# One encoder layer on eight cores: the order of all instructions fixed beforehand by a list scheduler, attention probabilities as the stationary operand, weights packed in blocks

## The chip, the cores and the metric

The kernel runs on all 8 cores of one Trainium2 chip, two dies of four cores each. Every core works on its own data; there is no collective. The time of an execution is the device time of the slowest core, in microseconds (us).

In some executions the cores of one die show a lower granted TensorE clock, and the time is longer.

## The reference

One layer of a streaming encoder. Core c handles prompt stream c (2048 tokens) and two running streams of 64 tokens each, 2176 tokens in all, with D = 1024, 16 heads of 64, and an FFN width of 2816.

```python
mod = silu(c) @ w_ada + b_ada                      # 9 vectors: shift, scale, gate
x = x + 0.5*gt1 * swiglu(modulate(rmsnorm(x)), w_ffn1_in, w_ffn1_out)
h = modulate(rmsnorm(x), ...); z = h @ w_in        # Q K V f B C X GA GC
logit[t,s] = q_t.k_s/8 + sum(log f_j, s < j <= t)  # causal, plus a cache of 1024 rows
o_attn = softmax(logit) @ v                        # for the two running streams
o_conv = B * short_conv(C * X, width 3)            # causal, per channel
m = sigmoid(GA)*o_attn + sigmoid(GC)*o_conv
x = x + gt2 * (m @ w_out)
x = x + 0.5*gt3 * swiglu(modulate(rmsnorm(x)), w_ffn2_in, w_ffn2_out)
y = rmsnorm(x)                                     # K, V, log f and conv states are outputs too
```

## The kernel before

The instructions of each engine are issued in the order in which the Python program emits them. Heads are handled in 8 pairs, and each pair c also owns 128 channels of the conv branch. The projections of the next pair and the conv work are "side" items, taken from a queue between the steps of attention (cuts are marked with `...`):

```python
def maybe_side():                     # called between the steps of attention
    ...
    while side_q and (n0 + (pushed[0] - p0) - len(side_q)) < int(2.4*nside*step[0]/88.0):
        side(1)

# scores: keys stationary; exp on ScalarE; P@V: V stationary, 512 query columns move
act(PT[pi][:, lo:512], PB[sb_][:, lo:512], AF.Exp, ..., bias=NF[...], scale=1.0)
mm([(PB[ob][:, lo:512], va[:, i, hh, :], PT[pi][:, lo:512], i == 0, i == ntile - 1)], ...)

def normalize(ob, ...):               # V has 64 ones columns, so rows 64..127 hold the sum
    act(LND[64:128, 0:ncol], PB[ob][64:128, 0:ncol], AF.Ln, ...)
    act(RD[64:128, 0:ncol], LND[64:128, 0:ncol], AF.Exp, ..., scale=-1.0)
    ...                               # VectorE: multiply, then times the gate

def sigmoid_split(dst, src_ps, ...):  # three ScalarE passes for each gate
    return [act(dst, src_ps, AF.Exp, scale=-1.0), act(dst, dst, AF.Ln, bias=1.0),
            act(dst, dst, AF.Exp, scale=-1.0)]

def wcols(w, c0, n):                  # a weight block: rows of 128 f32 = 512 bytes
    return w.rearrange("(k p) n -> p k n", p=128)[:, :, c0:c0 + n]
```

K and V outputs go through three staging buffers to DRAM. x is written to DRAM (xs) before attention and read back by five large loads after it.

The softmax here doesn't subtract the row's maximum and nothing guards it: scores larger than these inputs give would overflow.

## Time and profile before

The median is 2667.99 us of 3 executions (2651.4 to 2799.87; the last, 5.6% above the first, is a slow one). The profile is of core 1, span 2679.1 us.

These are lines of the page: the span, busy time and instruction counts of each engine, and the DMA packets.

```profile
span 2679.1 us, 35551 instructions; the slowest of 8 cores (2629.1 to 2679.1 us)
PE 2083.8 (78%) x11881; PEld 1013.9 (38%) x11881; DVE 920.9 (34%) x1566; ACT 967.3 (36%) x1948; POOL 258.9 (10%) x338
DMA packets 307537, 137.12 MB, mean 51 GB/s; under 512 B 255472, under 2 KB 278128, under 8 KB 307344
```

PE is TensorE, PEld its weight loads, ACT ScalarE, DVE VectorE. The next lines are windows of the same trace: start and end, length, busy time (and instructions) of each engine, mean granted clock of TensorE, share of the DMA engines, GB/s. They are the starved start of FFN 1, attention, the output projection, and FFN 2.

```profile
core 1: us, PE busy (x) PEld busy (x) DVE busy (x) ACT busy (x) POOL busy (x), PEclk, DMA share, GB/s
118.00:252.00 134.00, 118.86 (x986) 61.73 (x987) 23.32 (x46) 20.07 (x37) 58.54 (x70) 0.91 1.29 114
...
800.00:2000.00 1200.00, 864.49 (x5125) 435.20 (x5123) 476.87 (x833) 622.07 (x1312) 87.10 (x113) 0.84 0.37 34
2000.00:2140.00 140.00, 99.05 (x413) 41.48 (x414) 57.87 (x99) 57.04 (x102) 7.00 (x8) 0.84 0.52 92
2140.00:2600.00 460.00, 450.34 (x2384) 215.35 (x2382) 114.27 (x184) 68.45 (x126) 36.25 (x50) 0.99 0.26 34
```

Nearly half of the time is attention, where TensorE is busy 72% of the time and gets a clock of 0.84. What it waits for is in the list of TensorE's waits (engine, operand, line, what ended the wait: total us, times, longest):

```profile
PE pb L330 <- ACT RG L340: 125.9, 105, 6.2
...
PE pb L330 <- DVE stg L798: 67.5, 12, 25.2
...
PE pb L330 <- DMA wsall<-w_in: 44.4, 6, 11.4
```

The first are exponentials. `stg` are the staging buffers of K and V: a projection can't be drained until an earlier write to DRAM has landed. The list of DMA issues shows how late these writes and the weights land (last number: median us from issue to landing):

```profile
wsall<-w_in POOLq DMA_DIRECT2D x64, 256.0 KB, 14.2
...
wsall<-w1o POOLq DMA_DIRECT2D x22, 256.0 KB, 4.5
kT<-stg SPq DMA_DIRECT2D x22, 256.0 KB, 14.1
```

A w_in block has 512-byte rows and a w1o block 4 KB rows. Both are 256 KB, and the first takes three times as long (14.2 against 4.5 us). The loads convert 512-byte f32 rows to 256-byte bf16 rows, and 255472 of 307537 packets are under 512 B.

### The profile page before, as it was taken

To read this page: it belongs to the slowest core of one execution; us is meant where nothing else is said; L and a number is where in the kernel's file an instruction comes from. 1 tells how busy PE (TensorE), PEld (TensorE's weight loads), DVE (VectorE), ACT (ScalarE), POOL (GpSimd) and SP (SyncE) were. 2 spreads that over 40 slices of the span, in tenths; PEclk is the share of its full clock that TensorE was granted. 3 is DMA by queue.
4 is the path that set the end of the run, shared out by engine and by line. 5 is a ranking of instruction groups with operands and counts; after the bars stand their busy time and mean duration, and the time that the engine had idled before them with its cause. 6 is when DMAs were issued, how large, how long until landed. Compare 5 with 4: busy or idle time off the path is not lost.

```text
span 2679.1 us, 35551 instructions; the slowest of 8 cores (2629.1 to 2679.1 us)
## 1 busy us (share of the span) xinstructions
PE 2083.8 (78%) x11881; PEld 1013.9 (38%) x11881; DVE 920.9 (34%) x1566; ACT 967.3 (36%) x1948; POOL 258.9 (10%) x338
## 2 busy tenths in 40 slices
PE   1598999988477877766684677777857699999986
PEld 0244444433144343433333334343323344444433
DVE  0411232233554443343433344443334422222233
ACT  3611101123344646445362454636643411001111
POOL 2243011000010100000010000100010110010000
PEclk9898999998688887878887888888878899999988
DMA  9899316202563352626417342241236332162111
GB/s 188 81 127 129 47 17 62 33 32 80 48 75 37 23 59 18 57 22 31 37 20 54 17 42 33 26 57 18 21 64 125 32 40 32 16 60 32 20 63 71
DMA packets 307537, 137.12 MB, mean 51 GB/s; under 512 B 255472, under 2 KB 278128, under 8 KB 307344
## 3 DMA queue, kind: packets, MB, share of 16 engines
q0 software_dynamic: 260688, 80.79, 36.9%
q1 hardware_dynamic: 46672, 54.05, 6.4%
q8 instruction: 101, 1.65, 0.3%
q14 instruction: 76, 0.62, 0.1%
HBM read 179.70 MB, written 35.82 MB: 80 GB/s over the span
## 4 chain that ended last, share of the span: by engine, by line
PE 61%; DMA 14%; DVE 9%; ACT 8%; issue 6%; SPq 1%; DVEq 0%; ACTq 0%; POOL 0%; POOLq 0%
PE pb L330 61%; DMA kT<-stg 5%; ACT RG L340 4%; DMA kT<-wsall 3%; DVE tmp L441 3%; DMA wsall<-w_in 2%; DMA wsall<-w1i 2%; DMA RX<-xT 1%; ACT scr L340 1%; ACT RX L340 1%; ACT lnms L340 1%; DMA RX<-xs 1%; DVE RX L769 1%; DVE RX L492 1%; ACT H L340 1%
## 5 line engine op out<-in xcount | busy, mean ns | idle before, releaser
L330 PE MATMUL pb<-H,wsall 128*128 128x512 bf16 (+1 forms) x5800 | 1220.1, 363 | 122.4 <-DMA wsall<-w_in 44.4
L330 PEld LDWEIGHTS pb<-H,wsall 128*128 128x128 bf16 x5800 | 537.3, 101 | 706.9 <-issue 223.6
L330 PE MATMUL pb<-RG,wsall 128*128 128x512 bf16 (+2 forms) x2416 | 546.4, 368 | 125.4 <-DVE RX L492 46.8
L340 ACT ACTIVATE RG<-pb,NF 128x512 bf16<-128x512 f32 (+3 forms) x640 | 369.2, 626 | 301.8 <-PE pb L330 299.7
L330 PEld LDWEIGHTS pb<-RG,wsall 128*128 128x128 bf16 x2416 | 232.2, 103 | 402.9 <-issue 210.6
L340 ACT ACTIVATE scr<-pb 128x512 bf16<-128x512 f32 (+1 forms) x220 | 117.1, 533 | 718.6 <-PE pb L330 718.6
L475 DVE TENSOR_TENSOR RG<-pb,scr 128x512 bf16<-128x512 f32 (+1 forms) x220 | 134.1, 611 | 523.0 <-PE pb L330 509.9
L330 PE MATMUL pb<-RG,RX 128*128 128x64 bf16 (+4 forms) x592 | 137.5, 305 | 121.1 <-ACT RG L340 96.8
L492 DVE SCALAR_TENSOR_TENSOR RX<-pb,DER,RX 128x512 f32<-128x512 f32 (+1 forms) x192 | 112.6, 594 | 217.1 <-PE pb L330 213.8
L340 ACT ACTIVATE scr<-RX 128x512 bf16<-128x512 f32 (+1 forms) x160 | 81.8, 556 | 270.2 <-PE pb L330 224.5
L330 PE MATMUL pb<-wsall,H 128*128 128x128 bf16 x1088 | 87.6, 250 | 105.0 <-DVE stg L798 40.4
L319 POOL DMA_DIRECT2D wsall<-w_in x65 | 57.1, 884 | 908.9 <-PE pb L330 908.9
L330 PE MATMUL pb<-RX 65*128 65x64 bf16 (+4 forms) x592 | 129.7, 313 | 17.0 <-DVE RX L954 17.0
L330 PE MATMUL pb<-RX,wsall 65*128 65x512 bf16 (+1 forms) x336 | 119.0, 401 | 8.6 <-DVE RX L954 8.6
L330 PE MATMUL pb<-scr,ones_bf 128*128 128x512 bf16 (+1 forms) x160 | 59.4, 400 | 82.5 <-ACT scr L340 77.5
L330 PEld LDWEIGHTS pb<-wsall,H 128*128 128x128 bf16 x1088 | 80.9, 114 | 108.9 <-issue 107.5
L330 PEld LDWEIGHTS pb<-RG,RX 128*128 128x128 bf16 x592 | 46.7, 108 | 186.0 <-issue 171.6
L441 DVE SCALAR_TENSOR_TENSOR tmp<-RX,DER,pb 128x512 f32<-128x512 f32 (+1 forms) x144 | 85.2, 592 | 68.3 <-ACT pb L340 48.0
L903 DVE TENSOR_TENSOR tmp<-pb,tmp 64x64 f32<-64x64 f32 (+1 forms) x96 | 50.6, 527 | 144.1 <-ACT tmp L340 142.6
L340 ACT ACTIVATE H<-tmp,MOD 128x512 bf16<-128x512 f32 (+1 forms) x144 | 85.8, 597 | 33.2 <-DVE tmp L441 28.6
L340 ACT ACTIVATE RG<-pb,NFS 128x64 bf16<-128x64 f32 x288 | 87.0, 313 | 22.7 <-ACT RG L340 1.5
L340 ACT ACTIVATE lnms<-pb 64x64 f32<-64x64 f32 (+3 forms) x116 | 55.6, 479 | 97.8 <-PE pb L330 96.2
(90 smaller groups left out, 1189.3 us busy)
## 6 DMA issues: line engine op xcount, KB each, us to landing
wsall<-w_ada POOLq DMA_DIRECT2D x72, 256.0 KB, 18.2
wsall<-w_in POOLq DMA_DIRECT2D x64, 256.0 KB, 14.2
wsall<-w1i POOLq DMA_DIRECT2D x44, 256.0 KB, 10.5
wsall<-w2i POOLq DMA_DIRECT2D x44, 256.0 KB, 7.1
RX<-xT SPq DMA_DIRECT2D x4, 2048.0 KB, 27.8
xs<-RX SPq DMA_DIRECT2D x4, 2048.0 KB, 6.8
RX<-xs SPq DMA_DIRECT2D x4, 2048.0 KB, 29.0
wsall<-w1o POOLq DMA_DIRECT2D x22, 256.0 KB, 4.5
```

Source lines behind the costliest of these rows:

```text
L319: P.dma("gpsimd", lambda e, d=dst, s=src_ap: e.dma_start(out=d, in_=s), writes=[WSB[i]], sem=WSS[i])
L330: ins = e.matmul(o, lhsT=l, rhs=r, start=st, stop=sp)
L340: return P.op("scalar", lambda e: e.activation(out=out, in_=in_, func=func, **kw), reads=reads, writes=writes)
L441: P.op("vector", lambda e, k=k, i=i, lo=lo, ln_=ln_, seq=seq: e.scalar_tensor_tensor(out=TMP[i][:, lo:lo + ln_], in0=xv[:, k, t0 + lo:t0 + ...
L475: P.op("vector", lambda e, ia=ia, bb=bb, jj=jj, t0=t0, n=n: e.tensor_tensor(out=gv[:, jj, t0:t0 + n], in0=PB[bb][:, 0:n], in1=SAB[ia][:, 0 ...
L492: P.op("vector", lambda e, bank=bank, mo=mo, t0=t0, lo=lo, ln_=ln_, seq=seq: e.scalar_tensor_tensor(out=xv[:, mo, t0 + lo:t0 + lo + ln_], ...
L769: P.op("vector", lambda e, r0=r0, lo=lo, ln_=ln_: e.tensor_tensor(out=T1[r0:r0 + 64, lo:lo + ln_], in0=T1[r0:r0 + 64, lo:lo + ln_], in1=T2 ...
L903: P.op("vector", lambda e: e.tensor_tensor(out=TT[r0:r0 + 64, 0:ncol], in0=PB[ob][0:64, 0:ncol], in1=RD[64:128, 0:ncol], op=ALU.mult), rea ...
```

## The change

The intent is to let a planner find the overlap that was interleaved by hand, and to take work off ScalarE and the DMA queues. The diff has about 2480 lines; this is its core.

```diff
-def mm(items, reads, writes): return P.op("tensor", fn, reads, writes)   # issued as emitted
+n.prio = self.base + self.step * 1e-3 + (prio or 0.0)   # every operation is a node
+P.schedule()                                            # one fixed order for every engine
...
+for c in range(8):                     # smaller number = more urgent
+    P.at(300.0 + c*10 + 5); kvqga(c + 1)   # projections of the next pair
+    P.at(300.0 + c*10);     attend(c)
+    P.at(500.0 + c*10);     conv(c)
...
+p_a = Pool("a", banks[0:4], excl=True)     # PSUM: scores
+p_o = Pool("o", banks[4:6], excl=True)     # P@V
+p_p = Pool("p", banks[6:8], excl=True)     # every projection, and the transposes
...
-mm([(PB[ob][:, lo:512], va[:, i, hh, :], PT[pi][:, lo:512], ...)])       # V stationary
+mm([(ot.ap[:, s*66:s*66+65], pt.ap[:, s*128:(s+1)*128], va[:, i, hh, 0:65], ...)
+    for s in subs])                        # P stationary: 64 columns of V and one of 2.0
-act(..., AF.Ln, ...); act(..., AF.Exp, scale=-1.0)
+dve(reciprocal(...)); dve(tensor_tensor(...))           # normalisation on VectorE
-sigmoid_split(...)                                      # Exp, Ln, Exp
+act(..., AF.Tanh, scale=0.5)    # the ones column of 2.0 absorbs the factor 0.5
-P.dma("gpsimd", ... w_in.rearrange("(k p) n -> p k n", p=128)[:, :, c0:c0+128])
+P.dma("gpsimd", ... w_in[block])   # [64, 128, 1024], packed beforehand: 4 KB rows
```

How the planner places an operation: it keeps a modelled time for each engine, takes the most urgent operation that is ready, gives it a free slot of its pool, and advances the engine to the time when that slot is free:

```python
n = heapq.heappop(rdy[e])[2]            # most urgent ready operation of engine e
got, full = slot_for(n)                 # a slot that no tile holds; it may be free only later
...
st = max(avail[e], n.ready)
for t, s in zip(n.alloc, got):
    ...
    st = max(st, s.free_at)             # the engine waits for the slot
avail[e] = st + occ
```

x is still written to DRAM, and comes back as 40 small tiles just before each is used. The conv branch of a pair runs on TensorE's projection banks with this chain on VectorE for each block of 512 tokens: C times X, the three taps, times B, times the gate, add.

## The prediction

> **What bounds the kernel now.** By the busy-time windows of the profiled core (span 2679 us):
>
> | us | stage | PE busy | granted clock |
> |---|---|---|---|
> | 0-118 | loads, first norm | under half | 0.87-1.00 |
> | 118-587 | FFN 1 | 92-100% | 1.00 once fed |
> | 587-800 | its tail, gate sums, first K/V | 64% | 0.82 |
> | 800-2000 | attention, projections | 73% | 0.84 |
> | 2000-2140 | output projection | 75% | 0.83-0.89 |
> | 2140-2680 | FFN 2, tail | 92% | 0.81-0.99 |
>
> Where TensorE is fed, a matmul costs its columns: 16 of 128 columns took 0.89 us (56 ns each), eight of 64 took 0.23 us (29 ns each). Weight loads hide. [...] By this law before needs about 1825 us at full clock (estimate: 1779 us of columns, 11881 matmuls); some 850 us are waiting and the lower clock that goes with it. The waits of PE between 690 and 2000 us: exponentials 126 us, K/V staging buffers 133 us (12 to 25 us at a time at the start of a head pair, until their write to DRAM is done), w_in loads 44 us.
>
> **What changes.**
> - PE work barely shrinks. P-stationary P@V is 2176 matmuls of 65 columns, about 65 us at 29-30 ns, against 118 us before; token-major gate and transposes give some back. Estimate for after: 1780 us at full clock.
> - ACT loses the Ln/Exp normalisation (93 us) and three-pass sigmoids (about 130 us; one tanh pass, about 45, instead). Eight 64-column exponentials (313 ns each) become one of 512 plus a DVE add. I estimate ACT 505 us and DVE 445 us in attention, against PE 705: TensorE is the bound if the schedule feeds it.
> - Packed weights: a block with 512-byte rows lands in 14-18 us, one with 4 KB rows (w1o) in 4.5 us. This removes two waits of 23 and 25 us from the chain in FFN 1, the 44 us in attention, and the slow landing of the kT writes in the same queues (14 us).
> - Scheduling: norm, gate sums, first K/V, output projection and FFN 2's start overlap.
>
> **Sum of after** (estimates): start 72 (was 118); FFN 1 515 (about 570); attention and projections 830, namely 705 at clock 0.96 and 88% fed (about 1310 with the gate stage); output projection 80 (140); FFN 2 495 and tail 15 (540). Total about 2010 us.
>
> **Prediction.** 2010 us, 8 in 10 between 1920 and 2140. Faster by over 2%: 0.95; within 2%: 0.03; slower: 0.02.
>
> **What would show it right.** PE busy 88-92%; clock 0.95 or more in attention; attention 800-860 us; 65-column matmuls about 30 ns apart; no PE wait over 5 us on staging buffers; packets under 512 B nearly gone; first FFN matmul near 70 us.
>
> **What would make it wrong.** The order is fixed beforehand from modelled times that look short (0.60 us against 0.69 traced for 512 columns), so in-order queues may wait on each other and attention stay at 900 or more. Pairs of a weight load and a 65-column matmul might not sustain 30 ns. [...] The x reload and first w2i blocks could collide behind the output projection.

Two passages are cut: a formula for the spacing of matmuls and a risk about the clock. The sum: 72 + 515 + 830 + 80 + 495 + 15 = 2007, about 2010 us. "This law" is the measured cost before it (56 and 29 ns), and the estimates of TensorE's work follow from the traces.

In the kernel before, the median time from the start of one matmul to the start of the next is 216 ns after one of 512 columns (1444 of them, 252 to 587 us), 56 ns at 128, and 29 ns at 64 (589, from 800 to 2000 us); in the changed kernel it is also 216 and 56 ns (1821 and 443 of them, 98 to 530 us), and 30 ns at 65 columns (179, from 1003 to 1030 us). At these spacings, and those of the few other widths, the matmuls come to 1825 us before, 1780 us after and 705 us in the stage with attention (estimates); a column adds (216 - 56)/384 = 0.417 ns, which makes the 1779 us of its 4269264 columns. That weight loads hide is read from the same 56 ns: a weight load lasts 98 ns in this trace (median of the 1088 of those matmuls), and they still start 56 ns apart. The kT writes are not in the queue of the weight loads, as the prediction has it: the trace lists them under SP, the loads under GpSimd.

## The result, and the profile after

The changed kernel is correct and runs in 2174.45 to 2181.27 us in its three fast executions (median of all six 2197.55; the slow ones take 2213.83, 2321.31 and 2456.27). The ratio of fast runs to the fast runs of before is 0.8147 (95% interval 0.8078 to 0.8216). A ratio is the mean time of one kernel's fast runs over that of the other's of the same rounds, so not quite the ratio of the medians. Executions in which one die ran at a lower clock are left out of the means. The direction was right. The size was not: 2010 us was predicted, with 1920 to 2140 as the range, and the time is about 170 us above the prediction.

The page of the profiled core 0, the lines that answer to those of before:

```profile
span 2179.7 us, 38451 instructions; the slowest of 8 cores (2160.6 to 2179.7 us)
PE 1949.7 (89%) x14273; PEld 1052.6 (48%) x14273; DVE 837.1 (38%) x1592; ACT 755.4 (35%) x1425; POOL 163.1 (7%) x312
DMA packets 67460, 137.50 MB, mean 63 GB/s; under 512 B 8416, under 2 KB 12640, under 8 KB 65728
```

Its windows are FFN 1, the tail of FFN 1 with the norm, attention, the conv branch after attention, and FFN 2:

```profile
98.00:530.00 432.00, 429.78 (x2657) 213.50 (x2655) 112.33 (x200) 73.44 (x143) 55.73 (x103) 1.00 0.41 65
530.00:680.00 150.00, 124.40 (x684) 62.18 (x682) 72.19 (x120) 67.32 (x117) 11.45 (x18) 0.80 0.38 94
680.00:1275.00 595.00, 550.51 (x6392) 376.74 (x6392) 230.28 (x482) 398.31 (x772) 24.43 (x46) 0.95 0.25 56
1275.00:1570.00 295.00, 242.07 (x1243) 110.59 (x1241) 196.68 (x407) 22.35 (x47) 12.67 (x24) 0.98 0.13 22
...
1680.00:2060.00 380.00, 379.61 (x2074) 184.98 (x2073) 92.93 (x162) 59.12 (x117) 26.41 (x50) 1.00 0.22 37
```

The waits of TensorE and the landing times:

```profile
PE pb L646 <- DVE SC L1269: 47.8, 37, 2.5
PE pb L646 <- ACT SC L668: 34.8, 17, 13.8
PE pb L646 <- DVE RX L853: 31.3, 11, 6.3
```

```profile
WS<-w_ada POOLq DMA_DIRECT2D x72, 256.0 KB, 9.9
WS<-w_in POOLq DMA_DIRECT2D x64, 256.0 KB, 5.8
```

The waits on staging buffers and on w_in are gone from the head of the list. The longest entry is new: line 1269 is the VectorE multiplication by the conv branch's projection B, after which the bank of that projection is free. Set against the sum of the prediction, with boundaries read from the two traces (the predicted terms add up to 2007, which the prediction rounded):

| stage | before, us | predicted | after, us | after minus predicted |
|---|---|---|---|---|
| start to the first FFN matmul | 118 | 72 | 76 | +4 |
| FFN 1 and its tail | about 570 | 515 | 560 | +45 |
| gate sums, projections, attention, conv | about 1310 | 830 | 936 | +106 |
| output projection | 140 | 80 | 93 | +13 |
| FFN 2 and the final norm | 540 | 510 | 515 | +5 |
| sum | 2679 | 2010 | 2180 | +170 |

The largest row as one window:

```profile
636.00:1572.00 936.00, 833.16 (x7921) 510.81 (x7919) 451.40 (x923) 437.77 (x842) 41.50 (x74) 0.95 0.22 47
```

So 106 of the 170 us lie in one stage, and its two windows show a split that the prediction had not made. From 680 to 1275 us ScalarE is busy 398 of 595 us; from 1275 to 1570 us it is busy 22 of 295 us, and TensorE only 242. The conv branch, at priority 500, runs after attention: the first of its 40 blocks ends at 1272.5 us, and only the first steps of one block came earlier.

Within attention the mean hides a second split. These are the costliest groups of instructions in a stretch of 27 us (line, engine, operation, operands, shapes, count, then busy us and mean ns of one, then idle time before them):

```profile
L668 ACT ACTIVATE RG<-pb,NF 128x512 bf16<-128x512 f32 x40 | 24.5, 886 | 0.4 <-PE pb L646 0.4
L646 PE MATMUL pb<-RG 65*128 65x512 bf16 x40 | 14.5, 377 | 2.5 <-ACT RG L668 0.7
L646 PE MATMUL pb<-RG 128*128 128x65 bf16 x180 | 12.9, 192 | 0.0
...
L646 PE MATMUL pb<-maskneg,ident_bf 128*128 128x128 bf16 x16 | 3.5, 220 | 0.0
```

The windows of this stretch, and of one that lies between two such stretches:

```profile
1003.00:1030.00 27.00, 23.21 (x256) 14.11 (x252) 5.08 (x13) 27.00 (x52) 0.34 (x1) 1.00 0.21 41
...
820.00:840.00 20.00, 19.41 (x210) 13.26 (x208) 10.18 (x16) 6.39 (x14) 0.00 (x0) 1.00 0.16 61
```

ScalarE is busy for all 27.00 us of the first (1003 to 1030 us), and no projection runs in it: none of its 256 matmuls is on a weight block (WS). At the spacings measured where matmuls follow one another (216, 30 and 56 ns for 512, 65 and 128 columns, beside the prediction), the groups shown are 8.6 + 5.4 + 0.9 = 14.9 us of column time, and all 256 matmuls 16.7 us (an estimate). The busy time of TensorE in the stretch is 23.21 us, so the busy row does not show that it has room. Here the row is some 40% above the column time: matmuls overlap in it, since one of 65 columns is listed with 192 ns and the next starts 30 ns after it. At 820 to 840 us the opposite holds: the next pair's projections run, and ScalarE is busy 6.39 of 20 us.

The chain of waits in the conv tail shows one period, 8.13 us long (start, us, what; "issue" and queue entries in between left out):

```profile
1393.72 3.63 PE pb L646 x16
...
1397.51 0.70 DVE RG L1238
...
1398.74 0.40 DVE SC L1260
...
1399.23 0.76 DVE SC L1264
...
1400.09 0.76 DVE SC L1264
...
1401.01 0.70 DVE SC L1269
...
1401.85 1.24 PE pb L646 x5
```

A block of 512 tokens has four projections of 8 matmuls, about 6.9 us of columns (32 x 216 ns, an estimate). Only two banks serve them, and a bank comes free only after VectorE's chain, so TensorE waits about 1.1 us in every block, for line 1269.

### The profile page after: what moved, and what is told of

It is laid out like the page before. It is cut to its first block, busy times and chain, and to the rows that moved or that the text cites. A ratio compares the mean times of both kernels' runs of the same rounds, so it can differ in the third digit from the quotient of the medians.

```text
span 2179.7 us, 38451 instructions; the slowest of 8 cores (2160.6 to 2179.7 us)
## 1 busy us (share of the span) xinstructions
PE 1949.7 (89%) x14273; PEld 1052.6 (48%) x14273; DVE 837.1 (38%) x1592; ACT 755.4 (35%) x1425; POOL 163.1 (7%) x312
## 2 busy tenths in 40 slices
DMA packets 67460, 137.50 MB, mean 63 GB/s; under 512 B 8416, under 2 KB 12640, under 8 KB 65728
## 4 chain that ended last, share of the span: by engine, by line
PE 74%; DVE 10%; issue 6%; ACT 5%; DMA 4%; DVEq 0%; SPq 0%; ACTq 0%; POOLq 0%; POOL 0%
PE pb L646 74%; ACT RG L668 4%; DVE SC L1264 2%; DMA G<-g 1%; DVE SC L1269 1%; DVE RG L1238 1%; DVE SC L798 1%; ACT H L668 1%; ACT SC L668 1%; DMA BADA<-b_ada 1%; DVE SC L1260 1%; DVE SC L812 1%; DMA WS<-w_ada 0%; DMA yT<-SC 0%; DVE RX L853 0%
## 5 line engine op out<-in xcount | busy, mean ns | idle before, releaser
L646 PE MATMUL pb<-H,WS 128*128 128x512 bf16 (+2 forms) x5480 | 1059.2, 352 | 69.0 <-DVE SC L1269 47.8
L646 PEld LDWEIGHTS pb<-H,WS 128*128 128x128 bf16 (+1 forms) x5480 | 489.4, 99 | 599.9 <-issue 124.6
L646 PE MATMUL pb<-RG,WS 128*128 128x512 bf16 (+1 forms) x1888 | 366.6, 355 | 33.7 <-DVE RX L853 31.3
L668 ACT ACTIVATE SC<-pb 128x512 bf16<-128x512 f32 (+3 forms) x260 | 138.4, 533 | 716.8 <-PE pb L646 710.0
L837 DVE TENSOR_TENSOR RG<-pb,SC 128x512 bf16<-128x512 f32 (+1 forms) x220 | 134.5, 612 | 478.0 <-PE pb L646 463.7
L646 PEld LDWEIGHTS pb<-RG,WS 128*128 128x128 bf16 x1888 | 174.6, 101 | 223.4 <-issue 65.3
L646 PE MATMUL pb<-RG 128*128 128x65 bf16 (+4 forms) x1424 | 148.5, 236 | 15.8 <-ACT RG L668 4.8
L646 PE MATMUL pb<-WS,H 128*128 128x128 bf16 x2176 | 132.9, 222 | 5.3 <-DVE RG L680 4.1
L646 PE MATMUL pb<-RX 65*128 65x512 bf16 (+3 forms) x456 | 116.9, 317 | 18.0 <-ACT RG L668 4.9
L646 PEld LDWEIGHTS pb<-WS,H 128*128 128x128 bf16 x2176 | 126.3, 100 | 13.2 <-issue 11.6
```

What stands on the lines that cost most here:

```text
L646: ins = e.matmul(o, lhsT=l, rhs=r, start=st, stop=sp, skip_group_check=nogroup)
L668: return e.activation(out=out, in_=in_, func=func, **kw)
L837: dve(lambda e, n=n, tb=tb, jj=jj, sa=sa, pb=pb: e.tensor_tensor(out=gap(jj, tb), in0=pb.ap[:, 0:n], in1=sa.ap[:, 0:n // 2].bitcast(BF16), ...
```

## The experiments

Two theories compete for the missing 170 us. **Theory A, the order:** the work costs what the prediction said, but the fixed order separates work that needs ScalarE from work that doesn't, and holds TensorE for banks. **Theory B, the work:** TensorE really is occupied 92% of the attention phase; the P@V pairs cost 69 to 77 ns each, which is their busy time over their count, and not 30. Where an expectation uses other letters, it says what they stand for. All twelve kernels gave correct results. Of a time given for a run, fast executions alone count. Runs of one chip job are listed with the ratio to the kernel before on the same chip, since jobs differ: the mean of the fast runs of the kernel before was between 2663 and 2691 us in the four jobs of the experiments. In the job of experiments 4, 7 and 8, half of the eight executions of the kernel before were slow, and the record calls all four of its comparisons with that kernel unclear; they rest here on the fast runs that are listed.

### 1. The conv branch at the priority of its own pair

```diff
-            P.at(500.0 + c * 10)
+            P.at(300.0 + c * 10 + 7)
             conv(c)
```

> Edit: the scheduling priority of the conv branch of head pair c is raised from 500+10c (after everything of attention) to 307+10c (just after its own pair); nothing else. Theory A (two phases that each leave another engine idle: in the changed kernel attention runs at 33 to 100% ACT by turns from 680 to 1275 us, and the conv tail from 1275 to 1570 us leaves ACT at 8% and PE waiting on DVE): interleaved, the 936 us from the gate sums to the last conv shrink by 50 to 110 us, the separate low-ACT tail disappears, total 2060 to 2130 us. Theory B (TensorE bounds the attention phase, as its 92% busy says): the conv work only moves, total stays within 20 us of 2180.

Measured: 2100.6 to 2103.9 us, ratio 0.7885 (0.7843 to 0.7927), against 0.8147: 77 us less than after's 2178.9 us (the mean of its three fast runs). The tail without ScalarE is gone. From about 636 to 1495 us, attention and conv together take about 860 instead of 936 us. Moving nothing but the order gives back nearly half of the missing time, so Theory A holds for this part.

### 2. Every P@V matmul issued twice

```diff
-   (ot.ap[...], pt.ap[...], va[:, i, hh, 0:65], i == 0 and s == 0, i == nt-1 and s == 3) for s in subs],
+   (ot.ap[...], pt.ap[...], va[:, i, hh, 0:65], i == 0 and s == 0 and v_ == 0,
+    i == nt-1 and s == 3 and v_ == 1) for s in subs for v_ in (0, 1)],
```

The same was done for the running streams. Sums and weights double alike, so the result stays right; the planned order is the same.

> Edit: every P-stationary P@V matmul is issued twice (numerator and denominator double, the result stays right); the order on all engines is that of the changed kernel. Adds 2464 pairs of weight load and 65-column matmul. Theory A (a pair costs about 30 ns where TensorE is fed; the exponentials bound about half of the attention phase and hide it there): 15 to 50 us longer. Theory B (TensorE bounds attention and a pair costs the 77 ns that busy time divided by count gives): 150 to 190 us longer. A pair at 30 ns with TensorE the bound everywhere: about 75 us.

Measured: 2183.4 to 2189.6 us, ratio 0.8197; the page counts 16721 matmuls for 14273. The mean is 6 us above after's, 13 us by the ratios, which two jobs do not resolve. If 2448 more pairs cost almost nothing, TensorE is not the bound in attention, whatever its busy row says. One thing mixes in: the granted clock from 680 to 1275 us is 1.00 in this trace and 0.95 in the changed kernel's. At the measured spacings the changed kernel's 6392 matmuls there are 449 us of columns, and the 2315 more of this trace some 69 us at 30 ns; at a clock of 0.95 the old ones need 473, so the clock can have paid for some 24 of the added 69 us (an estimate), and idle time for the rest. Theory B, 150 to 190 us, falls here. It is also less than Theory A's own range allowed: I had expected that part of the pairs would show.

### 3. Every exponential of 512 columns as four of 128

```diff
+   w = n // parts                       # parts = 4 for the full 512-column tiles
+   for j in range(parts):
+       ins = e.activation(out=out[:, j*w:(j+1)*w], in_=in_[:, j*w:(j+1)*w], func=func, **kw)
```

> Edit: each of the 448 exponentials of 512 columns is issued as four of 128 columns (same result, same order), which adds only fixed cost on ACT: by the 0.38 us of an isolated 128-column one against 0.69 us of a 512-column one, and 0.53 us spacing in bursts, I estimate 0.15 to 0.35 us per tile, 70 to 150 us of ACT time in all. Theory A (ACT bounds about half of the attention phase): at least half of the added ACT time shows in the span, 40 to 130 us longer. Theory B (TensorE bounds it, ACT is idle a third of the phase): under 20 us.

Measured: 2362.9 to 2364.4 us, ratio 0.8867: 185 us more. ScalarE's busy time rises from 755.4 to 957.6 us, by 202 us, so some 90% of it shows in the time. This is more than expected: the expectation's 0.53 us is a mean over tiles of mixed width. Back to back, exponentials of 512 columns start 0.57 us apart in the changed kernel and those of 128 columns 0.25 us apart here, so a split adds 0.43 us, and 448 of them about 190 us. In the changed kernel, from 1003 to 1030 us, exponentials of 512, 384, 256 and 128 columns were followed by the next after 0.57, 0.46, 0.36 and 0.25 us; a line through these leaves 0.14 us that does not depend on the columns (an estimate), and a split adds three times that. Two lines of its windows, both in attention, and the head of TensorE's waits:

```profile
820.00:840.00 20.00, 16.10 (x109) 8.38 (x107) 1.03 (x3) 20.00 (x79) 0.00 (x0) 0.50 0.00 1
1020.00:1040.00 20.00, 16.15 (x111) 8.87 (x109) 0.61 (x2) 20.00 (x80) 0.00 (x0) 0.50 0.00 1
```

```profile
PE pb L646 <- ACT RG L672: 90.6, 286, 1.1
```

ScalarE is full, VectorE nearly idle, and TensorE follows one tile at a time, at half of its clock (0.50, where the changed kernel's stretch from 1003 to 1030 us had 1.00; what decides was not tested). Experiments 2 and 3 together settle what bounds attention in the changed kernel: in the exponential stretches it is ScalarE, and TensorE has room that the order leaves unused.

### 4. The planner no longer lets a tile hold TensorE for a bank

The planner's code offers a cause for the two kinds of stretch in attention. A score matmul has the higher priority, and it is ready. If its bank is free only when an exponential has read it, the planner still takes it and advances TensorE to that time. The less urgent projections then never see TensorE idle. The kernel issues the instructions in the planned order, so on the chip TensorE stands and waits as planned (16.7 us of columns in the 27 us from 1003 to 1030 us). Five lines put such an operation, on any engine, back until its slot is free:

```diff
+            hold = max([s.free_at for s in got], default=0.0)
+            if hold > max(avail[e], n.ready) + EPSI:
+                n.ready = hold
+                heapq.heappush(pend[e], (n.ready, n.idx, n))
+                continue
             st = max(avail[e], n.ready)
```

No operation is added, removed or made cheaper.

> Edit: five lines in the list scheduler of the kernel. When the PSUM bank (or buffer) that an instruction is to write comes free only later, the instruction is put back in the queue instead of taking the engine and holding it until then, so that lower-priority ready work can run. Priorities, pools and work unchanged. Theory A (in the exponential-bound stretches, 52 exponentials in 27.6 us in one example, the fixed order holds TensorE at a score matmul that waits for its bank, while projections are ready): the projections of the conv branch move into those stretches, the tail with ACT at 8% shrinks from 295 us to under 200, total 2010 to 2075 us. Theory B (the order is not at fault; the two banks of the projection pool are): within 25 us of 2180, since the pool is unchanged.

Measured: 2014.3 to 2024.6 us, ratio 0.7614 (0.7575 to 0.7653): 161 us less than the changed kernel. Its attention phase and its conv tail, as windows:

```profile
655.00:1125.00 470.00, 462.82 (x6288) 335.40 (x6286) 230.31 (x487) 391.40 (x754) 24.55 (x46) 1.00 0.32 71
1125.00:1430.00 305.00, 246.30 (x1253) 111.96 (x1253) 197.04 (x413) 23.61 (x49) 15.96 (x31) 0.95 0.15 22
```

The same work, about 6300 matmuls and 390 us of ScalarE, takes 470 instead of 595 us. The whole stage, from the gate sums to the last conv block (605 to 1426 us), takes 821 instead of 936 us, with TensorE busy 751.22 us at a clock of 0.98. Of the rest of the gain, 31 us lie before it (the gate sums start at 605 instead of 636 us) and 17 us after it. The groups of a stretch of 27 us (950 to 977 us) now hold exponentials and projections together:

```profile
L673 ACT ACTIVATE RG<-pb,NF 128x512 bf16<-128x512 f32 x23 | 14.3, 690 | 0.6 <-PE pb L651 0.6
L651 PE MATMUL pb<-RX,RG 128*128 128x65 bf16 x114 | 8.8, 193 | 0.0
L651 PE MATMUL pb<-WS,H 128*128 128x128 bf16 x127 | 8.1, 219 | 0.0
L651 PE MATMUL pb<-H,WS 128*128 128x512 bf16 x32 | 7.7, 378 | 0.0
```

One part of the expectation missed: the conv work did not move into attention, and the tail stayed at about 305 us with the same wait of TensorE on VectorE (the list of waits: 45.4 us in 35 times, for the line that was 1269). The next pair's projections alone were enough to fill the stretches.

### 5. The conv projections may also use the four score banks

```diff
+        p_c = Pool("c", banks[0:4] + banks[6:8], excl=True)
-                pc = proj(wC, tb, None, gate)
+                pc = proj(wC, tb, None, gate, p_c)      # and the same for X, B and the gate
```

This was run twice: alone, and on top of experiment 4.

> Edit: the conv projections may also use the four PSUM banks of the attention scores, which are idle in the tail (pool of 6 banks instead of 2); priority unchanged. Theory A (the period of 8.05 us per 512-token block of the tail is a loop through a bank: DVE frees a bank, PE computes two projections into it, 3.63 us, DVE runs six operations, 4.4 us, and frees the next): period near 7 us, its 32 matmuls' 6.9 us, so 30 to 40 us shorter, the 48 us of waits of PE on that DVE line gone. Theory B (the DVE operations themselves, 67% busy, bound the tail): under 10 us.

Measured alone: two of five executions were fast, 2067.5 and 2069.6 us, too few for an interval of the ratio. That is 110 us less than the changed kernel, where 30 to 40 were expected. More banks in the tail account for part of it only: 6 of the 40 blocks of conv work ended before 1250 us, since they could now get a bank during attention, and most of the rest ran from 1250 to 1450 us with TensorE busy 193.69 of 200 us.

> e8 (a tile waiting for a bank may no longer take TensorE in the list) gave 2017 us and left a conv-only tail of about 305 us (1125 to 1430) that turns once per 8 us over two projection banks. Here the conv projections may also use the four score banks. Theory A (the tail is a turnaround of two banks, TensorE waits for VectorE to free them): the tail's TensorE share rises from about 82% to over 93%, the tail shrinks by 35 to 60 us, and the total is 1950 to 1985 us. Theory C (the gain of the banks in e3 came from conv work moving into the attention stretches, which e8 already fills): 2000 us or more.

Measured on top of experiment 4: 1936.7 and 1939.0 us (the other two executions were slow), 80 us less than experiment 4. Its attention and tail:

```profile
650.00:1115.00 465.00, 461.10 (x6247) 334.56 (x6243) 231.08 (x487) 387.94 (x750) 24.45 (x46) 1.00 0.32 71
1115.00:1340.00 225.00, 216.41 (x1238) 107.28 (x1238) 163.46 (x358) 43.81 (x87) 12.69 (x24) 0.98 0.17 29
```

Attention is about as long as in experiment 4 (465 us), and the tail shrinks from 305 to 225 us, with TensorE at 96% instead of 81%. So the tail was the turnaround of two banks, and the gain here is the tail's. It was more than the 35 to 60 us expected.

### 6. Experiments 1 and 4 together

> e8 plus the conv branch at the priority of its pair (as in e1, which alone gave about -76 us). If the conv tail costs because ScalarE idles there while the attention stretches are full, mixing balances them: 1940 to 1990 us. If e8's filling and e1's reordering fill the same idle time, they do not add: 2000 to 2060 us.

Measured: 1949.9 to 1963.9 us, ratio 0.7265 (0.7213 to 0.7318), 63 us less than experiment 4 by the means. From 650 to 1350 us TensorE is busy 48 to 49 of every 50 us, and ScalarE between 19 and 43. The two ways to fix the tail, more banks and mixing, come within 20 us of each other.

### 7. The changed kernel with unpacked weights, and the kernel before with packed weights

```diff
-            w = wload(p_w, w_ada[kind * 8 + jj])
+            w = wload(p_w, w_ada.rearrange("(k p) n -> p k n", p=128)[:, :, j*128:(j+1)*128])
```

> Edit: w_ada, w1i, w_in and w2i are read from their unpacked row-major layout again (rows of 512 bytes per block instead of 4 KB), everything else as in the changed kernel. Theory A (packing removed what the weight loads cost: the starved first 100 us of FFN 1, the w_in waits): 40 to 120 us longer, most of it in the first 250 us, with waits of PE on w_ada and w1i. Theory B (the changed kernel's early prefetch into 16 slots hides slow loads as well): under 20 us.

Measured: 2200.5 to 2212.1 us, ratio 0.8317; 26 us more by the means, 2% (some 45 us) more by the ratios of the two jobs, so between the two theories or within A. Packets under 512 B rise to 237792, and a w_ada block lands in 16.3 us. TensorE waits 51.3 us for them where it waited 16.6; since its wait for the modulation additions behind the small loads falls from 19.4 to 4.3 us at the same time, the start is some 14 us later (first FFN matmul at 90.4 instead of 76.1 us), and not 35. The later loads are slow again too (w_in 9.5 us), but no wait of TensorE for them is in the list.

The reverse: only the packing, in the kernel before.

> Edit: the kernel before with only the packed weight layout added (one part of the change alone). Theory A (loads cost the kernel before about 48 us in FFN 1, 44 us of w_in waits and part of the 133 us of waits for K/V staging, whose kT writes share the DMA engines): 70 to 150 us shorter than before, kT landing well under 14 us. Theory B (those waits would be replaced by others, since attention there is bound by its own chain): 50 us or less.

Measured: 2547.1 to 2570.5 us, ratio 0.9663 (0.9546 to 0.9781): 90 us less by the ratio, 104 by the means. Two landing times of it:

```profile
wsall<-w_in POOLq DMA_DIRECT2D x64, 256.0 KB, 4.4
...
kT<-stg SPq DMA_DIRECT2D x22, 256.0 KB, 2.8
```

The K writes themselves did not change. They land in 2.8 instead of 14.1 us, and the wait on `stg` falls from 67.5 to 31.4 us. Only the weight loads changed, and the share of the DMA engines that their queue takes falls from 36.9% to 21.6%; that the writes waited behind them there is the likely reading. The same packing was worth about 100 us in the old kernel and 26 to 45 us in the new one, in which fewer late loads show as waits.

### 8. The small loads ahead of the activations

The chain of waits of the changed kernel starts with five small loads, one after another, because all five write one buffer object of the dependency tracker (13.12, 27.97, 7.64, 6.72 and 5.20 us), and the first VectorE addition of the modulation starts at 63.41 us. Here they go first and have five objects.

```diff
+for o_, i_, b_ in ((BADA, b_ada3, B_bada), (G3, g3, B_g3), (CW, conv_wT, B_cw), (SCT, scT, B_sct), (BFt, b_f, B_bf)):
+    P.dma("sync", ..., 65536, (), [b_])
 xload(0, 0)
-for o_, i_ in ((BADA, b_ada3), (G3, g3), (CW, conv_wT), (SCT, scT), (BFt, b_f)):
-    P.dma("sync", ..., 65536, (), [B_small])
```

> Edit: the five small constant loads (b_ada, g, conv weights, conv state, b_f) are issued before x and write five separate hazard buffers, not one, so that they don't wait for each other. Theory A (the chain of waits of the first 63 us is these five loads one after the other behind the 9 MB of x: 13, 28, 8, 7 and 5 us): the first modulation add falls from 63 us to 50 or less, then bounded by the last of the first 16 w_ada blocks (54 us), the first FFN matmul from 76 us to 55 to 65, total 10 to 20 us shorter. Theory B (all of the start is bound by the transfers of x and w_ada): under 5 us.

Measured: 2165.4 to 2175.0 us, ratio 0.8188. The mean is 8 us below the changed kernel's and the ratio is above it, so no gain is resolved. The chain says why:

```profile
22.40 35.53 DMA WS<-w_ada
57.93 0.14 issue
58.06 0.37 PE pb L646 x8
...
58.52 0.19 DVE MOD L764
```

With the small loads out of the way, the last modulation weights end the wait instead, and the first FFN matmul comes at 66.7 us in place of 76, a little later than the 55 to 65 expected. The wait had a second holder right behind the first.

### 9. Everything together, and the price of a pair where TensorE is the bound

Experiment 4, the banks of experiment 5 and the loads of experiment 8 in one kernel:

> e10 plus small loads ahead of the activations (e4 alone: about -8 us). If the parts add: e10 minus 5 to 10 us, 1940 to 1975 us, the fastest version. Rival: no difference from e10 within 4 us, because the last modulation weights bound the start in e4.

Measured: 1929.0 to 1956.4 us, six fast of seven (five of them within 1929.0 to 1930.9), ratio 0.7187 (0.7142 to 0.7232). This is the fastest version, 28% below the kernel before by the ratio. Against the two fast runs of the kernel with banks alone it is 8 us less by medians of the fast runs and 4 by means; whether the early loads matter stays open.

In this kernel TensorE is fed (busy 446.10 of 450 us from 650 to 1100 us, at a clock of 1.00), so doubling the P@V pairs again measures them:

> In e2, doubling the 2448 P@V pairs cost about 5 us, but there TensorE waited in the attention stretches, so the added pairs could hide. In e9 (1930 us) TensorE shows 99% busy from 650 to 1100 us, ScalarE about 82%. The same doubling on top of e9. Theory A (each pair costs its columns, 29 to 37 ns, when TensorE is the bound): 2448 x 29 to 37 ns = 71 to 91 us more, 2000 to 2021 us. Theory B (a pair has a larger fixed cost, the 69 to 77 ns that the busy time divided by the count suggests): 169 to 189 us more, 2100 us or more. If TensorE is still not the bound in e9's attention: under 50 us more, below 1980 us.

Measured: five fast executions from 1990.9 to 1992.3 us, ratio 0.7431 (0.7389 to 0.7473). The medians of the fast runs differ by 62 us, the ratios by 0.0244, which is 66 us of some 2690. Divided by 2448 pairs that is 25 to 27 ns each, where such pairs start 30 ns apart in the changed kernel (1003 to 1030 us) and the 65 columns alone are 27 ns at 0.417 ns each (an estimate, beside the prediction). It lies between two of the stated ranges, and far from Theory B's 169 us or more. The weight loads of the pairs are hidden: one lasts about 100 ns in the changed kernel's list (680 to 1275 us).

| kernel | fast runs, us | mean of fast runs | ratio to before |
|---|---|---|---|
| changed kernel | 2174.5 to 2181.3 | 2178.9 | 0.8147 |
| conv at its pair's priority | 2100.6 to 2103.9 | 2102.1 | 0.7885 |
| conv with six banks | 2067.5, 2069.6 | 2068.5 | too few fast |
| no holding for a bank | 2014.3 to 2024.6 | 2018.3 | 0.7614 |
| no holding, conv early | 1949.9 to 1963.9 | 1955.3 | 0.7265 |
| no holding, six banks | 1936.7, 1939.0 | 1937.9 | too few fast |
| no holding, six banks, small loads first | 1929.0 to 1956.4 | 1934.3 | 0.7187 |

## Why the prediction was right or wrong

**Right: the direction, and most of the mechanisms.** The packets under 512 B fell from 255472 to 8416, and experiment 7 shows what the packing is worth in each kernel. The staging waits are gone from the head of the list. TensorE is busy 89% (88 to 92 predicted), and its clock in attention is 0.95. The first FFN matmul came at 76 us, near 70. P-stationary pairs cost about their columns (experiment 9). FFN 2 and the start were within 5 us of the sum.

**Wrong: the step "attention and projections 830, namely 705 at clock 0.96 and 88% fed".** It is the largest miss: 936 us. The prediction added each engine's work over the whole stage, "ACT 505 us and DVE 445 us in attention, against PE 705", and concluded that "TensorE is the bound if the schedule feeds it". The 705 and the clock held: at the spacings measured in the trace the 7921 matmuls of the stage are 705 us of columns (an estimate), and the clock was 0.95. The factor that failed is "88% fed": 705/(936 x 0.95) is 79%. The busy row hides this, since it reads 833.16 of 936 us, 89%. In experiment 4 the same operations take 821 us, 705/(821 x 0.98) = 88% fed, and the total of 2014 to 2025 us lies at the predicted 2010. So what failed is the "if". The order splits the stage into pieces with different bounds: exponential stretches, where ScalarE is full and TensorE is held for a bank (experiments 2, 3 and 4); projection stretches, where ScalarE is mostly idle; and a conv tail of 295 us, where ScalarE is busy 8% and two banks turn round through VectorE (experiments 1 and 5). A sum over the stage sees none of this. Two facts pointed to it before the run: conv carries priority 500 in the diff, behind every head pair, and TensorE's pool for all projections has two banks. The prediction costs neither.

**The warning was right for the wrong reason.** The prediction named a bad order as a way to fail ("in-order queues may wait on each other and attention stay at 900 or more"), because the plan's 0.60 us for an exponential looked shorter than 0.69 us in the trace. That is not what happened: from 1003 to 1030 us exponentials of 512 columns started 0.57 us apart (0.69 us is how long one lasts alone, and they overlap), so the plan did not err in that direction. The planner planned the wait itself, and the range should have been wider above.

**Mis-sized: FFN 1, +45 us, and the output projection, +13 us.** The fed part of FFN 1 is as expected (429.78 of 432 us busy). The excess is in the tail from 530 to 680 us, at clock 0.80. The list of waits puts 15.9 us of it on the addition into x (line 853). Experiment 4 bears on it: with the holding gone, FFN 1 and its tail take 529 us instead of 560, the wait on that line is 3.1 us from 500 to 660 us, and the clock from 530 to 655 us is 0.96. So the holding, or what it brought with it, made some 31 of the 45 us. The other 14 us, and the output projection, were not tested.

**The clock with all cores at work.** In the profiled fast execution the fed stretches of FFN 1 and FFN 2 (98 to 530 and 1680 to 2060 us) ran at 1.00 on all eight cores. One die ran at 0.79 to 0.80 in one slow execution (a mean over the whole of it).

## What to carry to other kernels

When a fixed order replaces hand interleaving, do not add up engine times over a stage: list, for each stretch, which engine is full and whether work for the others is allowed to run there, and look first at what runs last. A list scheduler must not let an urgent operation take an engine while it waits for a buffer; five lines that put it back were worth 161 us here, nearly the whole gap to the prediction. To test whether a busy engine is the bound, double its work in place: the same 2448 pairs cost about 6 us where TensorE was being held and 62 us where it was fed. Compare the granted clocks as well: in the first of these two, attention ran at 0.95 without the added pairs and at 1.00 with them.
